# Low parts handed round between DMA, GpSimd and VectorE, and a first norm without GpSimd

## The chip, the cores and the metric

One core of a Trainium2 chip runs the whole program. The metric is device time in microseconds, the median of three runs. A core has five engines with a queue each: TensorE (PE, matrix products), VectorE (DVE), ScalarE (ACT), GpSimd (POOL) and SyncE (SP, which here only issues transfers); sixteen DMA engines carry the transfers.

## The reference

A trunk of two layers over 256 tokens of width 1024, in float32. Each layer does, with shift, scale and gate vectors from a conditioning vector c:

```
mod = silu(c) @ w_mod[l] + b_mod[l]                 # 6 vectors of 1024
h = rms_norm(x, norm1_g[l]) * (1.0 + sc1) + sh1
x = x + g1 * hybrid_mixer(h, ...)                   # attention, two convolutions, spatial gating; w_in, w_out
h = rms_norm(x, norm2_g[l]) * (1.0 + sc2) + sh2
x = x + g2 * peer_ffn(h, wq, keys, u, v)            # top 16 of 16384 experts per head, 8 heads
```

`peer_ffn` is computed densely: gelu(h @ u) for all 16384 experts, times gates that are zero for experts not picked, times v. Each layer reads 64 MB of u and 64 MB of v for it. A last rms_norm follows.

## The kernel before, in words

**Tiles and parts.** All weights come as a stream of 128x1024 tiles of 512 KB (20 of w_in, 8 of w_out, 16 of wq, 128 of u and 128 of v a layer). TensorE multiplies in a rounded float32 format, so each tile is split into a high part (its rounding) and a low part (the rest), and each product is made of three: high by high, high by low and low by high (`mm3`, lines 362 to 364). The activations are split in the same way. A tile of u, w_in or wq takes 8 chunks x 3 = 24 matmuls of 256 columns (`products`), a tile of v 12 of 512 columns (`down`, line 928).

**The stream** (`Stream`, lines 154 to 217). `load` issues the transfer of a tile from SP into one of four buffers `raw` (line 175). `split_halves` splits half a tile at a time, 128x512, into `hi` and `lo`, six buffers each. The low part is made in one of three ways. By VectorE or GpSimd: ScalarE writes the high part (line 200), and the engine subtracts it from raw (line 202). By DMA: ScalarE writes the negated high part into `lo` (line 196), GpSimd issues a transfer that adds the raw tile onto it (line 197), and ScalarE writes the high part (line 198). Which way a tile goes is set by `share`, a dictionary of fractions that are summed up tile by tile; what is left goes to VectorE. After the second half of tile n is split, `load(n + 4)` is called; that transfer waits until nothing reads the buffer of tile n any more. `ahead` keeps the splitting five halves ahead of the products.

**Shares.** The mixers and the query projection use `MIXSHARE` (DMA 0.4). `SHARE` has four entries for the expert stage: the first 64 tiles of u, the second 64, the first 64 tiles of v, the second 64 (`experts`, lines 954 to 969).

**Work beside the products.** `Background` holds generators, and after each tile `pump` takes slices from them as long as a plan of VectorE's load allows (2.6 us of plan for each tile, line 933 and others; a low half on VectorE is charged with 0.6, line 204). In the first half of "up" these are the top-k search of the experts (`topk`; line 799 adds two score lists, 792 is its last search step, 815 to 821 build one-hot tables), and in layer 0 then 16 modulation tiles. In the second half of "up" and in "down" the gates follow (`gates`, line 879), and in layer 0 during "down" 40 modulation tiles of layer 1. The framework's own scheduler orders each engine's instructions afterwards, so the order of issue is not that of the source.

**Modulation** (`mod_tiles`, lines 273 to 295). The vectors are sums along rows: a 128x1025 tile of w_mod is loaded by SP (line 280), and VectorE multiplies it by silu(c) and sums it (line 286). `n` buffers are used in turn; a slice of the generator is one sum.

**The start** (`start`, lines 1021 to 1084). The first norm needs the statistics of x (`rstd_d`) and 16 modulation tiles, taken one by one. GpSimd multiplies x by the reciprocal root (line 1060), ScalarE applies scale and shift twice, once rounded (1067) and once not (1069), and GpSimd subtracts (1073); the last chunk goes by VectorE. The first two weight tiles have their low parts made by DMA (`share = {"dma": 1.0}`, `split(1)`). In the later norms (`norm_mod`, lines 348 to 353) VectorE scales (350), ScalarE rounds (351) and VectorE makes the low part (352).

Of the kernel before, what the change touches and what calls it, by code (L numbers as in the profile page):

```python
# [10 lines left out]
F32 = mybir.dt.float32  # L11
# [3 lines left out]
AF = mybir.ActivationFunctionType  # L15
ALU = mybir.AluOpType
# [4 lines left out]
T = 256  # L21
L = 2
NC = D // P
# [14 lines left out]
MODCOST = 1.2  # L38
LOCOST = 0.6
HALF = D // 2  # L40
# [5 lines left out]
KTAKE = 3  # L46
CONVRANK = 2.5
PACE = (1.0, 2.6)
SHARE = ({"dma": 0.3, "pool": 0.7}, {"dma": 0.25}, {"dma": 0.2}, {"dma": 0.1})
NCOL = 94  # L50
NROW = 64 + 256 + 256 + 128
CH_SLICES = (4, 3, 0, 1, 7, 6, 5)
# [101 lines left out]
class Stream:  # L154
# [24 lines left out]
    def split_halves(self, upto):  # L179
        nc = self.nc  # L180
        while self.ns <= min(upto, 2 * len(self.aps) - 1):
            n, k = divmod(self.ns, 2)
            if k == 0:
                self.load(n)
                self.parts[n] = ([], [])
                self.by = "dve"
                for way in ("dma", "pool"):
                    self.acc[way] += self.share.get(way, 0.0)
                    if self.by == "dve" and self.acc[way] >= 1.0:
                        self.acc[way] -= 1.0  # L190
                        self.by = way
            raw = self.raw[n][:, HALF * k:HALF * k + HALF]
            hi = self.pool.tile([P, HALF], F32R, name="hi", tag="hi", bufs=6)
            lo = self.pool.tile([P, HALF], F32R, name="lo", tag="lo", bufs=6)
            if self.by == "dma":
                nc.scalar.activation(out=lo, in_=raw, func=AF.Copy, scale=-1.0)  # L196
                nc.gpsimd.dma_start(out=lo, in_=raw, accum_op=ALU.add)  # L197
                nc.scalar.activation(out=hi, in_=raw, func=AF.Copy)  # L198
            else:
                nc.scalar.activation(out=hi, in_=raw, func=AF.Copy)  # L200
                eng = nc.gpsimd if self.by == "pool" else nc.vector
                eng.tensor_tensor(out=lo, in0=raw, in1=hi.bitcast(F32), op=ALU.subtract)  # L202
                if self.by == "dve":
                    self.bg.charge(LOCOST)
            self.parts[n][0].append(hi)
            self.parts[n][1].append(lo)
            self.ns += 1
            if k:
                del self.raw[n]
                self.load(n + self.depth)  # L210
# [9 lines left out]
class Trunk:  # L220
# [52 lines left out]
    def mod_tiles(self, l, chunks, sc, bufs, tail=True, pace=0.0):  # L273

        nc = self.nc
        n = len(bufs)

        def load(i):
            if i < len(chunks):
                nc.sync.dma_start(out=bufs[i % n], in_=self.io["wmod"][l, chunks[i]])  # L280

        for i in range(n - 1):
            load(i)
        for i, j in enumerate(chunks):
            w = bufs[i % n]
            nc.vector.scalar_tensor_tensor(out=w, in0=w, scalar=1.0, in1=sc, op0=ALU.mult, op1=ALU.mult,  # L286
                                           accum_out=self.modT[:, l, j:j + 1])
            load(i + n - 1)
            yield MODCOST, pace
        for j0 in (8, 32):  # L290
            if tail and j0 in chunks:
                m = self.modT[:, l, j0:j0 + 8]
                g = self.col(l, 0 if j0 == 8 else 8, 8)
                nc.vector.scalar_tensor_tensor(out=m, in0=m, scalar=1.0, in1=g, op0=ALU.add, op1=ALU.mult)
                yield 0.2
# [64 lines left out]
    def mm3(self, out, whi, wlo, hhi, hlo, start, stop):  # L360
        mm = self.nc.tensor.matmul
        mm(out, whi, hhi, start=start, stop=False)  # L362
        mm(out, whi, hlo, start=False, stop=False)  # L363
        mm(out, wlo, hhi, start=False, stop=stop)  # L364
# [574 lines left out]
    def experts(self, l, area):  # L939
# [13 lines left out]
        acts = [self.big(32, T) for _ in range(2)]  # L953
        self.stream.share = SHARE[0]
        run = self.up(hb, acts)
        next(run)
        self.stream.share = SHARE[1]
        acts += [self.big(32, T) for _ in range(2)]
# [5 lines left out]
        for i in range(2):  # L964
            self.bg.add(self.gates(1, acts[2:4], i, kept))
        self.stream.share = SHARE[2]
        run = self.down(acts)
        next(run)
        self.stream.share = SHARE[3]
        self.m = Carve(self.big(), self.big())  # L970
# [50 lines left out]
    def start(self):  # L1021

        nc, io, one = self.nc, self.io, self.one
        self.cols = one.tile([P, L * NCOL + 8], F32, name="cols")
        self.ident = one.tile([P, P], F32, name="ident")
        self.xT = one.tile([P, NC, T], F32, name="xT")
        self.ones = one.tile([P, P], F32, name="ones")
        self.eps = one.tile([P, 1], F32, name="eps")
        self.iota = one.tile([P, P, 2], FP16, name="iota")
        self.modT = one.tile([P, L, 48], F32, name="modT")  # L1030
        self.idx = one.tile([P, 2, T], FP16, name="idx")
        self.gidx = one.tile([P, 2 * T], FP16, name="gidx")
        nc.vector.memset(self.ones, 1.0)
        nc.vector.memset(self.eps, EPS)
        self.neghalf = one.tile([P, 8], F32, name="neghalf")
        nc.vector.memset(self.neghalf, -0.5)
        self.m = m = Carve(self.big(), self.big())
        self.m2 = Carve(self.big())
        row = m.take(D)
        nc.sync.dma_start(out=row[0:1], in_=io["crow"])  # L1040
        nc.sync.dma_start(out=self.cols, in_=io["cols"])
        for i in range(2):
            nc.sync.dma_start(out=self.xT[:, 4 * i:4 * i + 4], in_=io["xT"][:, 4 * i:4 * i + 4])
        cr = self.m2.take(D + 1)
        for i in range(2):
            b = self.bank()
            nc.tensor.matmul(b, self.ones[0:1], row[0:1, 512 * i:512 * i + 512], start=True, stop=True)
            nc.scalar.activation(out=cr[:, 512 * i:512 * i + 512], in_=b, func=AF.Silu)
        nc.vector.memset(cr[:, D:D + 1], 1.0)
        bufs = [self.m2.take(D + 1) for _ in range(6)]  # L1050
        mods = self.mod_tiles(0, [j for c in range(NC) for j in (c, 8 + c)], cr, bufs, tail=False)
        next(mods)
        rs = self.rstd_d(m)
        self.stream.depth = 0
        self.stream.share = {"dma": 1.0}
        self.stream.split(1)
        r = self.bias_rows()
        xa, a = m.take(NC, T), m.take(2, T)
        for c in range(NC):
            nc.gpsimd.tensor_tensor(out=xa[:, c], in0=self.xT[:, c], in1=rs, op=ALU.mult)  # L1060
        hhi, hlo = hb = [self.mid(NC, T, dt=F32R) for _ in range(2)]
        for c in range(NC):
            for _ in range(2 if c else 1):
                next(mods)
            sh, sc = self.modT[:, 0, c:c + 1], self.modT[:, 0, 8 + c:9 + c]
            nc.vector.tensor_scalar(out=sc, in0=sc, scalar1=1.0, scalar2=self.col(0, c, 1), op0=ALU.add, op1=ALU.mult)
            nc.scalar.activation(out=hhi[:, c], in_=xa[:, c], func=AF.Identity, scale=sc, bias=sh)
            if c < NC - 1:
                nc.scalar.activation(out=a[:, c % 2], in_=xa[:, c], func=AF.Identity, scale=sc, bias=sh)
            else:  # L1070
                nc.vector.tensor_scalar(out=a[:, c % 2], in0=xa[:, c], scalar1=sc, scalar2=sh, op0=ALU.mult, op1=ALU.add)
            eng = nc.gpsimd if c < NC - 1 else nc.vector
            eng.tensor_tensor(out=hlo[:, c], in0=a[:, c % 2], in1=hhi[:, c].bitcast(F32), op=ALU.subtract)  # L1073
        for _ in mods:
            pass
        self.stream.load(3)
        self.stream.depth = self.stream.RAW
        nc.sync.dma_start(out=self.ident, in_=io["consts"][:, 0:P])
        m.reset()
        self.bias = m.take(4, 256)  # L1080
        self.table = self.bg.add(self.bias_table(r), rank=-1)
        self.bg.pump(0.1)
        self.mods = self.mod_tiles(0, list(range(16, 40)), cr, bufs[0:WBUFS])
        return hb
# [101 lines left out]
```

## Time and profile before

| | |
|---|---|
| median of 3 runs | 2087.24 us (2086.33 to 2091.59) |
| profiled execution | 2079.62 us, span 2077.8 us, mean granted clock 0.961 |
| busy share of the span | PE 92%, PE weight load 83%, DVE 69%, ACT 56%, POOL 26% |
| low parts | DMA 290 halves, GpSimd 178, VectorE 732 |
| DMA | 485.59 MB, 234 GB/s; q1 (plain loads) 56.9% and q0 (GpSimd's) 20.9% of 16 engines |

A busy share is a mean over stages with different limits; the stages are told apart by windows, given in us from the start of the span. In a wait, "A <- B" says that A was idle until B was done. "Up" is the product with u, "down" that with v.

### The profile page before, as it was taken

The page shows a single profiled execution, that of the slowest core. Times are in us where ns is not written, and L with a number is a line of the kernel's source. Part 1 is how long each engine was busy: PE and PEld are TensorE (multiplying, and loading weights), DVE is VectorE, ACT ScalarE, POOL GpSimd, SP SyncE. Part 2 cuts the span into 40 slices and gives each one's busy share as a digit, 9 for nine tenths or more (in the row PEclk, how much of TensorE's full clock was granted, in tenths as well). Part 3 has the DMA queues.
Part 4 walks back from the last instruction along what each step waited for, and adds up shares of the span by engine and source line. Part 5 has one row for each costly group of instructions (what it writes and reads, how often), then busy time and mean ns, then how long its engine had stood idle before and what let it go on. Part 6 is the DMA issues. An engine that isn't in the chain of part 4 may idle for free. (4 is left out here: it accounts for less than half of the span.)

```text
span 2077.8 us, 38198 instructions
## 1 busy us (share of the span) xinstructions
PE 1908.0 (92%) x13718; PEld 1720.2 (83%) x13718; DVE 1432.6 (69%) x3280; ACT 1155.0 (56%) x2329; POOL 537.2 (26%) x513
## 2 busy tenths in 40 slices
PE   4877987899999998889999989999999999999998
PEld 3777887889999886667787889999999988878886
DVE  6787799344666687666557877993477668855555
ACT  4565653465555554444557776666555555555554
POOL 4121265772111110000002223777411111110001
PEclk7988998899999999999999999999999999999999
DMA  8886877887888888898766767887888788877673
GB/s 289 256 254 204 223 198 223 260 229 218 249 244 255 255 256 287 279 295 284 225 211 168 206 167 204 238 219 219 234 262 243 245 255 271 261 207 220 210 212 113
DMA packets 164735, 485.59 MB, mean 234 GB/s; under 512 B 18588, under 2 KB 19905, under 8 KB 164290
## 3 DMA queue, kind: packets, MB, share of 16 engines
q1 hardware_dynamic: 122786, 407.13, 56.9%
q0 software_dynamic: 41760, 76.04, 20.9%
q8 instruction: 107, 1.75, 0.3%
q14 instruction: 82, 0.67, 0.1%
HBM read 388.72 MB, written 18.36 MB: 196 GB/s over the span
## 5 line engine op out<-in xcount | busy, mean ns | idle before, releaser
L364 PE MATMUL bank<-mid,lo 128*128 128x256 f32 x2432 | 702.3, 289 | 61.1 <-DMA lo<-raw 59.1
L200 ACT ACTIVATE hi<-raw 128x512 fp32r<-128x512 f32 x910 | 543.6, 624 | 323.4 <-PE bank L363 192.5
L362 PE MATMUL bank<-mid,hi 128*128 128x256 f32 x2432 | 704.5, 290 | 13.5 <-ACT hi L200 6.7
L363 PE MATMUL bank<-mid,hi 128*128 128x256 f32 x2432 | 695.5, 286 | 8.9 <-POOL mid L1073 8.9
L202 DVE TENSOR_TENSOR lo<-raw,hi 128x512 fp32r<-128x512 f32 x732 | 485.0, 688 | 204.5 <-ACT hi L200 200.1
L197 POOL DMA_DIRECT2D lo<-raw x290 | 253.2, 894 | 1390.6 <-PE acc L928 651.6
L928 PE MATMUL acc<-hi,mid 128*128 128x512 f32 x2048 | 570.0, 396 | 0.1
L364 PEld LDWEIGHTS bank<-mid,lo 128*128 128x128 f32 x2432 | 474.8, 195 | 72.0 <-DMA lo<-raw 69.2
L362 PEld LDWEIGHTS bank<-mid,hi 128*128 128x128 f32 x2432 | 475.1, 196 | 18.1 <-ACT hi L200 7.1
L363 PEld LDWEIGHTS bank<-mid,hi 128*128 128x128 f32 x2432 | 475.3, 196 | 9.5 <-POOL mid L1073 9.2
L928 PEld LDWEIGHTS acc<-hi,mid 128*128 128x128 f32 x2048 | 386.2, 191 | 78.4 <-ACT mid L913 0.4
L928 PE MATMUL acc<-lo,mid 128*128 128x512 f32 x1024 | 328.4, 398 | 31.5 <-DMA lo<-raw 31.2
L913 ACT ACTIVATE mid<-big 128x256 fp32r<-128x256 f32 x256 | 106.0, 415 | 307.8 <-PE acc L928 307.2
L928 PEld LDWEIGHTS acc<-lo,mid 128*128 128x128 f32 x1024 | 195.0, 190 | 84.5 <-DMA lo<-raw 44.2
L202 POOL TENSOR_TENSOR lo<-raw,hi 128x512 fp32r<-128x512 f32 x178 | 249.9, 1516 | 45.1 <-ACT hi L200 42.1
L198 ACT ACTIVATE hi<-raw 128x512 fp32r<-128x512 f32 x290 | 181.3, 625 | 134.7 <-PE bank L363 65.3
L914 DVE TENSOR_TENSOR mid<-big,mid 128x256 fp32r<-128x256 f32 x256 | 107.8, 423 | 199.0 <-PE acc L928 143.2
L196 ACT ACTIVATE lo<-raw 128x512 fp32r<-128x512 f32 x290 | 179.4, 621 | 57.8 <-PE acc L928 50.1
L286 DVE SCALAR_TENSOR_TENSOR big<-big 128x1025 f32<-128x1025 f32 x96 | 128.9, 1352 | 64.1 <-DMA big<-wmod 56.5
L874 DVE TENSOR_TENSOR og<-o,gidx 128x512 f16<-128x512 f16 x256 | 101.5, 436 | 0.2
L898 ACT ACTIVATE big<-bank 128x256 f32<-128x256 f32 x256 | 93.9, 367 | 0.0
L879 PEld LDWEIGHTS <-o 128*128 128x128 f16 x2048 | 67.4, 97 | 18.6 <-issue 12.3
(203 smaller groups left out, 1617.0 us busy)
## 6 DMA issues: line engine op xcount, KB each, us to landing
raw<-u SPq DMA_DIRECT2D x256, 512.0 KB, 4.6
raw<-v SPq DMA_DIRECT2D x256, 512.0 KB, 4.4
lo<-raw POOLq DMA_DIRECT2D x290, 256.0 KB, 5.0
big<-wmod SPq DMA_DIRECT2D x96, 512.5 KB, 6.5
raw<-win SPq DMA_DIRECT2D x40, 512.0 KB, 4.7
raw<-wq SPq DMA_DIRECT2D x32, 512.0 KB, 4.4
kept<-o SPq DMA_DIRECT2D x64, 256.0 KB, 5.2
o<-kept SPq DMA_DIRECT2D x64, 256.0 KB, 4.5
```

Source lines behind the costliest of these rows:

```text
L196: nc.scalar.activation(out=lo, in_=raw, func=AF.Copy, scale=-1.0)
L197: nc.gpsimd.dma_start(out=lo, in_=raw, accum_op=ALU.add)
L198: nc.scalar.activation(out=hi, in_=raw, func=AF.Copy)
L200: nc.scalar.activation(out=hi, in_=raw, func=AF.Copy)
L202: eng.tensor_tensor(out=lo, in0=raw, in1=hi.bitcast(F32), op=ALU.subtract)
L286: nc.vector.scalar_tensor_tensor(out=w, in0=w, scalar=1.0, in1=sc, op0=ALU.mult, op1=ALU.mult, accum_out=self.modT[:, l, j:j + 1])
L362: mm(out, whi, hhi, start=start, stop=False)
L363: mm(out, whi, hlo, start=False, stop=False)
L364: mm(out, wlo, hhi, start=False, stop=stop)
L913: nc.scalar.activation(out=a[:, 0], in_=src, func=AF.Copy)
L914: nc.vector.tensor_tensor(out=a[:, 1], in0=src, in1=a[:, 0].bitcast(F32), op=ALU.subtract)
L928: nc.tensor.matmul(self.acc[2 * tt + d], a[:, s, P * tt:P * tt + P], w[:, 512 * d:512 * d + 512], start=i == 0 and s == 0 and w is whi, st ...
```

## The change

Four edits. The shares of the expert stage change. A low part made by DMA adds the tile as it lies in HBM (`self.aps[n]`), not the raw buffer. In `mod_tiles` the load of a later tile is issued after the `yield`, so with the next slice. And the first norm is written like the later ones, VectorE scaling and making the low part, ScalarE rounding, with the shift added on the way; the first two weight tiles are loaded ahead and split inside its loop over the eight chunks, after chunks 2 and 4, with no share, so by VectorE.

```diff
-SHARE = ({"dma": 0.3, "pool": 0.7}, {"dma": 0.25}, {"dma": 0.2}, {"dma": 0.1})
+SHARE = ({"pool": 0.6}, {"dma": 0.25}, {"dma": 0.15}, {})
...
                 nc.scalar.activation(out=lo, in_=raw, func=AF.Copy, scale=-1.0)
-                nc.gpsimd.dma_start(out=lo, in_=raw, accum_op=ALU.add)
+                nc.gpsimd.dma_start(out=lo, in_=self.aps[n][:, HALF * k:HALF * k + HALF], accum_op=ALU.add)
                 nc.scalar.activation(out=hi, in_=raw, func=AF.Copy)
...
                                            accum_out=self.modT[:, l, j:j + 1])
+            yield MODCOST, pace
             load(i + n - 1)
-            yield MODCOST, pace
...
-        self.stream.share = {"dma": 1.0}
-        self.stream.split(1)
+        self.stream.share = {}
+        self.stream.load(1)
         r = self.bias_rows()
-        xa, a = m.take(NC, T), m.take(2, T)
-        for c in range(NC):
-            nc.gpsimd.tensor_tensor(out=xa[:, c], in0=self.xT[:, c], in1=rs, op=ALU.mult)
+        a = m.take(2, T)
...
-            nc.scalar.activation(out=hhi[:, c], in_=xa[:, c], func=AF.Identity, scale=sc, bias=sh)
-            if c < NC - 1:
-                nc.scalar.activation(out=a[:, c % 2], in_=xa[:, c], func=AF.Identity, scale=sc, bias=sh)
-            else:
-                nc.vector.tensor_scalar(out=a[:, c % 2], in0=xa[:, c], scalar1=sc, scalar2=sh, op0=ALU.mult, op1=ALU.add)
-            eng = nc.gpsimd if c < NC - 1 else nc.vector
-            eng.tensor_tensor(out=hlo[:, c], in0=a[:, c % 2], in1=hhi[:, c].bitcast(F32), op=ALU.subtract)
+            t = a[:, c % 2]
+            nc.vector.scalar_tensor_tensor(out=t, in0=self.xT[:, c], scalar=sc, in1=rs, op0=ALU.mult, op1=ALU.mult)
+            nc.scalar.activation(out=hhi[:, c], in_=t, func=AF.Identity, bias=sh)
+            if c in (2, 4):
+                self.stream.split(c // 2 - 1)
+            nc.vector.scalar_tensor_tensor(out=hlo[:, c], in0=t, scalar=sh, in1=hhi[:, c].bitcast(F32), op0=ALU.add,
+                                           op1=ALU.subtract)
```

## Rows read from the trace of the kernel before

**Rows 1.** Windows by stage: us, busy us (instructions) by engine, clock, DMA share, GB/s

```profile
254.00:371.00 117.00, 98.28 (x737) 95.72 (x736) 111.12 (x318) 55.42 (x112) 70.16 (x59) 0.91 0.74 217
371.00:483.00 112.00, 97.22 (x759) 95.80 (x758) 39.30 (x44) 60.32 (x117) 79.55 (x67) 0.94 0.82 233
784.00:985.00 201.00, 174.41 (x819) 137.41 (x818) 139.34 (x277) 93.89 (x188) 15.52 (x18) 0.93 0.88 289
1281.00:1378.00 97.00, 94.62 (x783) 93.77 (x782) 93.70 (x320) 60.08 (x116) 71.80 (x63) 1.00 0.82 226
1378.00:1477.00 99.00, 93.49 (x758) 92.37 (x757) 51.06 (x53) 60.72 (x117) 77.09 (x63) 0.98 0.82 226
1477.00:1690.00 213.00, 211.51 (x2126) 209.44 (x2125) 136.34 (x286) 119.48 (x237) 34.93 (x39) 1.00 0.81 248
1783.00:1941.00 158.00, 156.34 (x805) 126.70 (x804) 95.36 (x186) 89.45 (x183) 15.70 (x18) 1.00 0.76 224
```

**Rows 2.** Windows, two stretches in which TensorE has no gap

```profile
1425.00:1445.00 20.00, 19.96 (x165) 19.65 (x165) 4.05 (x5) 13.67 (x29) 16.06 (x14) 1.00 0.81 220
1950.00:2000.00 50.00, 50.00 (x219) 40.79 (x219) 29.40 (x53) 28.64 (x59) 3.08 (x4) 1.00 0.72 212
```

**Rows 3.** TensorE's waits, layer 0, first half of "up": total us, times, longest

```profile
PE bank L364 <- DMA lo<-raw: 25.4, 13, 5.8
PE bank L362 <- ACT hi L200: 6.7, 2, 5.1
```

**Rows 4.** TensorE's waits, layer 1, first half of "up"

```profile
PE bank L364 <- DMA lo<-raw: 7.7, 7, 2.0
```

**Rows 5.** Waits of all engines in the stretch of layer 0's "down"

```profile
PE acc L928 <- DMA lo<-raw: 26.6, 17, 3.6
DVE big L286 <- DMA big<-wmod: 26.6, 18, 4.1
```

**Rows 6.** Line 197 in that stretch: its issues, and its transfers

```profile
L197 POOL DMA_DIRECT2D lo<-raw x18: 859/862/877, 792.8 to 961.0; - x18
...
DMA to landing us min/median/max: 5.0/8.0/9.4
```

**Rows 7.** SP's waits, whole span

```profile
SPq L175 <- DMA lo<-raw: 693.4, 132, 13.4
```

**Rows 8.** SP's waits, first 32 tiles of layer 0's "up"

```profile
SPq L280 <- DVE big L792: 31.1, 3, 17.2
```

**Rows 9.** Line 286 (modulation sums), layer 0's "down": ns min/median/max, first and last start

```profile
L286 DVE SCALAR_TENSOR_TENSOR big<-big x40: 1217/1222/1229, 792.3 to 985.5; 128x1025 f32<-128x1025 f32 x40
```

**Rows 10.** Line 350 (scaled norm, 128x256), both layers

```profile
L350 DVE SCALAR_TENSOR_TENSOR big<-xT,modT,big x24: 475/479/484, 198.9 to 1247.5; 128x256 f32<-128x256 f32 x24
```

**Rows 11.** Page, part 5: low halves on VectorE: busy us, mean ns, idle before

```profile
L202 DVE TENSOR_TENSOR lo<-raw,hi 128x512 fp32r<-128x512 f32 x732 | 485.0, 688 | 204.5 <-ACT hi L200 200.1
```

**Rows 12.** TensorE's timeline at the start: start us, us, [idle before <-releaser]

```profile
31.89 0.58 PE L363 MATMUL bank<-mid,hi 128*128 128x256 f32 x1 [8.94 <-POOL mid L1073]
38.19 0.58 PE L364 MATMUL bank<-mid,lo 128*128 128x256 f32 x1 [5.71 <-DMA lo<-raw]
```

**Rows 13.** ScalarE's timeline: first activation of the first product

```profile
48.72 0.38 ACT L627 ACTIVATE big<-bank 128x256 f32<-128x256 f32 x1 [4.81 <-PE bank L364]
```

**Rows 14.** GpSimd's timeline: four low halves, layer 1

```profile
1294.79 5.35 POOL L202 TENSOR_TENSOR lo<-raw,hi 128x512 fp32r<-128x512 f32 x4
```

**Rows 15.** VectorE's timeline: the top-k addition alone and beside them

```profile
1292.16 0.41 DVE L799 TENSOR_TENSOR big<-big 128x256 f32<-128x256 f32 x1
...
1295.76 4.67 DVE L799 TENSOR_TENSOR big<-big 128x256 f32<-128x256 f32 x1
```

**Rows 16.** Groups of VectorE, layer 1, first half of "up"

```profile
L799 DVE TENSOR_TENSOR big<-big 128x256 f32<-128x256 f32 x16 | 34.2, 2139 | 0.0
```

**Rows 17.** Line 197, layer 1, second half of "up": who waited, and landing

```profile
  PE bank L364: 1.4, 3
...
DMA to landing us min/median/max: 3.3/5.3/6.9
```

## The prediction

> **What bounds the kernel now.** I first read the window table by stage: TensorE's busy time, the granted clock and the DMA share of each stretch, one layer beside the other, since both do the same products. [rows 1] holds the stretches that differ. The first half of the expert up-projection (64 tiles, cut here at the 32nd tile's activation) takes 117 + 112 = 229 us in layer 0 and 97 + 99 = 196 us in layer 1. A stretch of some 56 tiles of the down-projection (819 and 805 matmuls) takes 201 us in layer 0 and 158 us in layer 1. The second half of the up-projection has TensorE busy in 211.5 of 213 us. What is the least? Where TensorE runs without a gap, 165 products of 256 columns take 20 us and 219 of 512 columns take 50 us [rows 2]: 0.121 us and 0.228 us each, so an up tile (24 products) takes 2.91 us, a down tile (12) 2.74 us, and 64 up tiles 186 us. So layer 1 is bound by TensorE almost everywhere (196 against 186), and layer 0 loses 43 us in the first half of "up" and 43 us in the down stretch. That is what a change can win.
>
> Next the table of waits, by window, says what TensorE waited for there: in layer 0's half "up" 25.4 us for low parts that a DMA makes and 6.7 us for high parts [rows 3], in layer 1 7.7 us [rows 4]; in the down stretch 26.6 us for low parts by DMA, 17 times [rows 5], which is nearly each of the 18 halves made so there; they landed after 8.0 us in the median [rows 6]. The granted clock of 0.93 [rows 1] means 14% of 201 us at the lower of its two levels (1.2 of 2.4 GHz), half of which, 14 us, is lost: 26.6 + 14 explains the 43. Last come the waits of SP, whose queue issues all plain loads in order: 693.4 us in 132 waits for a raw tile that a low-part DMA still reads [rows 7], and, in layer 0's half "up", 31.1 us in three waits of a modulation load for a top-k step on VectorE (L792), all tile loads being queued behind it [rows 8].
>
> **The change, part by part.** The sum is made against the profiled execution, 2079.62 us, which lies 7.6 us under the median of 2087.24; I add these 7.6 at the end.
>
> *Start.* VectorE takes over all of the norm. Its work from 8.70 us on: 16 sums over modulation tiles at 1.22 [rows 9] and 0.08, 16 operations on 128x256 at 0.48 [rows 10] (eight scaled, eight low parts), 4 low halves at 0.69 [rows 11], and 4 us of reciprocal, copy and scales: 20.8 + 7.7 + 2.8 + 4 = 35.3, and about 2.7 of waiting for the statistics, less some 3 of overlap between neighbours. The last low part is out near 43.7 us, six products and the activation follow, near 45.5. Today the first product waits 8.94 us for GpSimd's low part and 5.71 us for the DMA's [rows 12], and its activation starts at 48.72 [rows 13]. I take -3 (between -6 and +2, since VectorE becomes the only bound).
>
> *First half of "up", low parts from DMA 0.3 / GpSimd 0.7 to GpSimd 0.6 / VectorE 0.4.* The waits for DMA go: 25.4 and 7.7. What is late next? GpSimd does four halves in 5.35 us [rows 14], so 1.34 each: its load falls from 0.7 x 2 x 1.34 + 0.3 x 2 x 0.86 (issue, [rows 6]) = 2.4 us to 1.6 us a tile of 2.91, and no longer bounds. VectorE gets 51 halves a layer. In the first 32 tiles it is already busy 93.7 of 97 us [rows 1] with top-k, and its queue is in order: a low half stands behind the top-k steps issued before it, and TensorE waits for it once the lead of five halves (5 x 1.45 = 7 us) is used up. The 26 halves there cost 26 x 0.69 = 18 us [rows 11], and each may wait for the port: a 128x256 addition of 0.41 us took 4.67 us [rows 15] while GpSimd ran its four halves, and 2.14 us in the mean of 16 [rows 16], 1.73 above 0.41. So the wait w per half lies between 0 and 1.7; I take 0.5, nearer to 0, since GpSimd has pauses at 1.6 of 2.91 us where today it runs in chains. The 16 additions then get 16 x 1.2 = 20 us back. VectorE needs 93.7 + 18 + 13 - 20 = 105 us, against 32 x 2.91 = 93 and 7 of lead: 5 us late. In the second 32 tiles VectorE is busy 51 of 99 us, so the halves fit, but they stand behind one-hot steps of 2 to 3 us in a row; I add one lead, 7. Drag: 12 us a layer. Its ends: 0 (w = 0), and 57 + 7 = 64 (w = 1.7).
> The Trainium skill (SBUF — State Buffer, section Who interferes with whom) says that a VectorE instruction with two SBUF inputs and a GpSimd instruction that reads SBUF take a port by turns, the later one blocking for the length of the other. By that, w would stay under one GpSimd half and average about 0.4, the drag would be 7, and the sum 10 us lower. The trace shows a wait through a chain of four, longer than the rule, so I keep the row.
> Layer 0: 186 + 6.7 + 4 (half clock around these waits) + 12 = 209, so -20. The SP stall stays in it (no load of the first three moves), but with VectorE and TensorE tied together it should not grow. Layer 1: 186 + 2 + 12 = 200, so +4.
>
> *Down, DMA 0.2 / 0.1 to 0.15 / 0.* In the stretch of rows 5 the first 32 tiles keep 4.8 DMA tiles, the other 24 have none: 10 halves of 18. Waits 26.6 x 10/18 = 15, clock 14 x 10/18 = 8: 18 us gained. The DMA engines (0.88 busy, [rows 1]) lose 8 slow halves of work and raw tiles come free earlier: 6 more. -24, between -8 (the 40 modulation loads in this stretch only fill the room) and -43 (all of layer 1's speed). VectorE takes these halves at 0.69 us; it is busy 139 of 201 us, which hides it. The rest of both down stages: -2.
>
> *The DMA reads the tile from HBM, not from the raw buffer.* 172 of 290 halves stay with DMA (0.4 x 44, 0.25 x 64 and 0.15 x 64 tiles a layer). A raw buffer is free once ScalarE has copied it, so SP's 693 us shrink; TensorE sees little of that, since it waits 1.4 us in all of layer 1's second "up" half [rows 17]. But the load that was held back until the low part had landed now runs beside it. Best, the waits of these stages that are left, some -30; worst, every later half of 81 tiles waits as in rows 5, 1.5 us: +121. The row nearest is that of the same stage: landing up to 6.9 us with 1.4 us of waits [rows 17]; a little later does little. I take +5.
>
> *Modulation loads issued after the yield.* One slice later in SP's order, ahead of the next sum. Queued behind a load that waits are the tile loads; behind a sum that waits, VectorE's low parts. Sums waited 26.6 us for loads in the down stretch [rows 5], with VectorE idle 62 us there: 0, between -10 (less blocking of SP) and +27 (the waits double and reach TensorE).
>
> Sum: -3 - 20 + 4 - 24 - 2 + 5 = -40. 2079.6 - 40 + 7.6 = 2047 us.
>
> **The rivals.**
> *All covers hold.* No drag, no collision, and the down stretch becomes like layer 1's: -5 at the start, 229 + 196 - 2 x 188 = -49, -43, and -6 elsewhere: -103, 1984 us. For it: GpSimd's relief; against: VectorE full for 97 us.
> *The port makes it slower.* VectorE's halves wait as the additions do today. Each 0.1 us of w costs (26 + 16) x 0.1 = 4.2 us a layer, 8.4 in both, so from w = 1.0 on the gain is gone. At 1.25, half way to the row's end, +63: 2110 us; at 1.7, 2150. For it: [rows 15, 16]; against: GpSimd's load falls by a third.
> *Low parts by DMA land later* because raw loads run beside them and the second read is a read of HBM under 250 GB/s. If a third of the 162 halves outside the down stretch waits 1.5 us: +80, 2127 us. For it: 8.0 us of landing where traffic is dense [rows 6]; against: 5.3 us in "up" [rows 17]. The Trainium skill (HBM Reference, section Latency) puts an access at 0.2 us on average and at 2 us under high load; by its upper figure such a half would land at 7.3 us and most would be late by little. No run here shows it.
> *Nothing moves.* The order in which instructions are issued is not that of the source (the 40 modulation sums that the code adds after tile 64 of "down" begin at 792 us, [rows 9], some 30 tiles earlier), so the redistribution may only trade DMA waits for VectorE waits: w = 1.0, 2089 us.
>
> **How the numbers follow.** Forecast 0.55 (2047, its own range 2015 to 2072), all covers 0.13, nothing moves 0.13, the port 0.11, DMA later 0.08. The bound between a change and none is 0.3%, 6 us: 2081 to 2093.5. Of "nothing moves" 0.09 lies inside and 0.02 on either side. Faster 0.55 + 0.13 + 0.02 = 0.70, same 0.09, slower 0.19 + 0.02 = 0.21. The range 2000 to 2105 leaves out about 0.09 below and 0.11 above.
>
> **What would show it.** Right: the first activation of the first layer near 45.5 us; no wait for DMA low parts in the first half of "up", layer 0's half near 209 us and layer 1's near 200; the down stretch near 177 us with its clock above 0.96; SP's waits for low parts by DMA under a third. Wrong: TensorE waiting for VectorE's low parts by more than 30 us a layer, the 128x256 additions still at 2 us, low parts by DMA landing at 7 us or more in the second half of "up", or the down stretch still near 200 us.

## The result, and the profile after

The kernel became slower: 2113.79 us (median of 4 runs, 2103.76 to 2122.67) against 2087.14 us, a ratio of 1.012 with a 95% interval of 1.007 to 1.017. The forecast was 2047 us, in a range of 2000 to 2105: wrong in sign, and outside its range. The profiled execution of after is its slowest one, 2122.67 us with a span of 2120.9, which is 43.1 us over the span before; the medians differ by 26.7.

First the same stages as in [rows 1], after. The columns are start and end, length, TensorE's busy time, weight loads, VectorE, ScalarE, GpSimd, the granted clock, the DMA share and GB/s.

```profile
240.00:448.00 208.00, 191.83 (x1533) 188.49 (x1532) 184.63 (x413) 100.66 (x197) 125.80 (x76) 0.98 0.60 204
768.00:955.00 187.00, 166.66 (x795) 133.42 (x795) 141.11 (x272) 88.38 (x178) 8.86 (x11) 0.95 0.87 295
1278.00:1480.00 202.00, 188.30 (x1531) 185.53 (x1529) 152.13 (x380) 101.32 (x197) 115.61 (x77) 0.99 0.51 169
1480.00:1701.00 221.00, 205.68 (x2032) 201.34 (x2031) 136.62 (x285) 112.33 (x220) 25.90 (x30) 0.98 0.78 227
1701.00:1920.00 219.00, 199.62 (x1250) 159.14 (x1247) 143.22 (x320) 101.52 (x208) 16.56 (x20) 0.95 0.68 204
```

The first three are the stages that the change was aimed at. Layer 0's first half of "up" takes 208 us (forecast 209), layer 1's takes 202 (forecast 200): so far the forecast holds. The down stretch takes 187 (forecast 177, before 201), some half of the gain that was forecast. The last two rows are stages in which I had expected next to nothing. Layer 1's second half of "up" took some 201 us before between the same two activations, bound by TensorE ([rows 1] has a longer cut of it, 213 us); it now takes 221. The first half of its "down" took 187 and now takes 219, with the clock down from 1.00 to 0.95. These two alone lose 52 us. The first half of layer 1's "down" in the kernel before:

```profile
1690.00:1877.00 187.00, 185.54 (x1236) 150.21 (x1236) 138.83 (x314) 102.71 (x212) 21.99 (x26) 1.00 0.82 246
```

TensorE's longest waits, whole span (total us, times, longest):

```profile
PE acc L928 <- DMA lo<-v: 41.9, 23, 3.7
PE bank L364 <- DVE lo L202: 30.4, 28, 3.5
PE bank L364 <- DMA lo<-u: 22.5, 20, 3.0
PE bank L364 <- DMA lo<-win: 13.1, 7, 5.7
PE bank L364 <- DMA lo<-wq: 10.2, 6, 4.9
```

Four of the five rows are low parts made by DMA, 87.7 us in 56 waits (smaller rows bring it to 93.3 us in 60). They bear the names of the weights (u, v, win, wq), since the transfer now reads those in HBM. What does the transfer itself look like? Line 197 in the last two stages above, first "up", then "down": who waited for it, and the time from issue to landing, as in [rows 17].

```profile
L197 POOL DMA_DIRECT2D lo<-u x30: 862/862/865, 1490.6 to 1689.6; - x30
...
  PE bank L364: 14.2, 11
...
DMA to landing us min/median/max: 3.8/6.3/9.3
```

```profile
L197 POOL DMA_DIRECT2D lo<-v x20: 862/865/1219, 1704.6 to 1919.9; - x20
...
  PE acc L928: 15.8, 10
...
DMA to landing us min/median/max: 3.5/7.0/8.6
```

In "up" the median landing rose from 5.3 to 6.3 us and the longest from 6.9 to 9.3, and TensorE's waits rose from 1.4 us in 3 to 14.2 in 11. (These two rows follow the transfers that were issued in the window; counted by the time of the wait, as in the table of stages below, it is 15.1 in "up" and 13.5 in "down".) One microsecond was the whole slack.

Last, the wait that the new source was to take away, in SP's queue [rows 7]:

```profile
SPq L175 <- DVE lo L202: 987.9, 361, 12.8
SPq L175 <- POOL lo L202: 95.3, 44, 5.0
SPq L175 <- ACT lo L196: 81.8, 41, 3.7
```

It is gone: no row names a DMA's low part. SP now waits until VectorE has read the raw tile, and no longer until the DMA has. And the second read of 172 halves (172 x 262,144 bytes = 45.1 MB) shows in the page, first before, then after:

```profile
HBM read 388.72 MB, written 18.36 MB: 196 GB/s over the span
```

```profile
HBM read 433.81 MB, written 18.36 MB: 213 GB/s over the span
```

### The profile page after: what moved, and what is told of

Read it like the earlier page. It is cut to its first block, busy times and chain, and to the rows that moved or that the text cites. A ratio compares the mean times of both kernels' runs of the same rounds, so it can differ in the third digit from the quotient of the medians.

```text
span 2120.9 us, 37761 instructions
## 1 busy us (share of the span) xinstructions
PE 1930.9 (91%) x13718; PEld 1736.4 (82%) x13718; DVE 1509.3 (71%) x3438; ACT 1101.6 (52%) x2208; POOL 417.5 (20%) x354
## 4 chain that ended last, share of the span: by engine, by line
PE 40%; issue 23%; DMA 13%; DVE 12%; POOL 1%; ACT 1%; POOLq 0%; DVEq 0%; SPq 0%; ACTq 0%
PE acc L928 17%; PE bank L364 7%; DMA lo<-u 7%; PE bank L362 7%; PE bank L363 7%; DMA lo<-v 3%; DVE lo L202 2%; DMA lo<-wq 1%; DMA lo<-win 1%; POOL lo L197 1%; DVE big L789 1%; PE acc L879 1%; DVE big L818 1%; DVE big L790 1%; DVE big L792 1%
## 5 line engine op out<-in xcount | busy, mean ns | idle before, releaser
L202 DVE TENSOR_TENSOR lo<-raw,hi 128x512 fp32r<-128x512 f32 x876 | 610.7, 721 | 287.4 <-ACT hi L200 282.7
L928 PE MATMUL acc<-hi,mid 128*128 128x512 f32 x2048 | 577.2, 400 | 0.1
L928 PEld LDWEIGHTS acc<-hi,mid 128*128 128x128 f32 x2048 | 391.1, 193 | 80.6 <-ACT mid L913 0.4
L202 POOL TENSOR_TENSOR lo<-raw,hi 128x512 fp32r<-128x512 f32 x152 | 244.1, 1618 | 177.1 <-ACT hi L200 157.0
L286 DVE SCALAR_TENSOR_TENSOR big<-big 128x1025 f32<-128x1025 f32 x96 | 123.6, 1293 | 38.8 <-DMA big<-wmod 38.6
L197 POOL DMA_DIRECT2D lo<-u x66 | 57.1, 865 | 381.5 <-ACT lo L196 193.1
L196 ACT ACTIVATE lo<-raw 128x512 fp32r<-128x512 f32 x172 | 105.8, 621 | 28.3 <-PE acc L928 25.0
L197 POOL DMA_DIRECT2D lo<-v x40 | 34.6, 872 | 431.9 <-PE acc L928 331.9
L874 DVE TENSOR_TENSOR og<-o,gidx 128x512 f16<-128x512 f16 x256 | 96.4, 417 | 0.2
```

The lines of the kernel that those rows point to most:

```text
L197: nc.gpsimd.dma_start(out=lo, in_=self.aps[n][:, HALF * k:HALF * k + HALF], accum_op=ALU.add)
L928: nc.tensor.matmul(self.acc[2 * tt + d], a[:, s, P * tt:P * tt + P], w[:, 512 * d:512 * d + 512], start=i == 0 and s == 0 and w is whi, st ...
```

## The experiments

My theory after the result: the place from which the low-part DMA reads costs some 70 us, and the rest of the change gains about what was forecast. The rivals were that VectorE and GpSimd hold each other up (theory 2 in the expectations), or that the new start or the moved modulation loads cost something (theory 3 is the loads). All ratios are against the kernel before, run on the same chip in turn (its medians: 2089.65, 2086.4 and 2089.39 in the three groups).

### One part alone, and the change without it

**The source alone** (`src_alone`): the kernel before, with only line 197 changed, so that all its 290 halves by DMA read HBM.

```
-                nc.gpsimd.dma_start(out=lo, in_=raw, accum_op=ALU.add)
+                nc.gpsimd.dma_start(out=lo, in_=self.aps[n][:, HALF * k:HALF * k + HALF], accum_op=ALU.add)
```

> Only the source of the adding transfers is changed (HBM instead of the raw buffer), all 290 halves. Theory 1 (the second read from HBM makes these halves land later and TensorE waits for them): landing in the second half of up from 5.3 to 6.4 us or more, TensorE's waits for low parts by DMA from 97 us to 150 or more, time 2110 to 2160. Theory 2 (the redistribution pushes low parts and gates back on VectorE, the source costs nothing): 2075 to 2095, waits as before. Theory 3 (the modulation loads): 2087.

**The change without it** (`undo_src`): the same line, the other way round, in the kernel after.

> The changed kernel with the source put back to the raw buffer, the other three edits kept. Theory 1: the loss of the second half of up (+20 in layer 1) and of the first half of down (+32 in layer 1) goes, 2035 to 2065, about what was forecast without a cost of the source. Theory 2: it stays, 2100 to 2115. Theory 3: it stays too.

**The redistribution alone** (`share_alone`), and **the first norm alone** (`start_alone`, the start block of the diff), each in the kernel before:

```
-SHARE = ({"dma": 0.3, "pool": 0.7}, {"dma": 0.25}, {"dma": 0.2}, {"dma": 0.1})
+SHARE = ({"pool": 0.6}, {"dma": 0.25}, {"dma": 0.15}, {})
```

> Only the four shares are changed, source still the raw buffer. Theory 1: first half of up in layer 0 from 229 to about 208 us, in layer 1 about +5, down in layer 0 shorter by 15 to 25: 2045 to 2075. Theory 2: 2100 to 2120, with waits of TensorE for VectorE's low parts above 30 us and a slower second half of up. Theory 3: 2045 to 2087.

> Only the first norm is changed. All theories: first product's activation 3 to 5 us earlier, 2078 to 2086; if the gain of the first mixer (18 us by its last matmul in the changed kernel) is due to the start, 2065 to 2075.

Measured (us):

| kernel | median | range | ratio (95%) |
|---|---|---|---|
| src_alone | 2226.66 | 2214.77–2232.87 | 1.065 (1.060–1.069) |
| undo_src | 2044.62 | 2039.97–2049.75 | 0.977 (0.973–0.982) |
| share_alone | 2062.32 | 2055.20–2071.09 | 0.986 (0.982–0.990) |
| start_alone | 2078.07 | 2067.89–2087.03 | 0.994 (0.991–0.997) |

The source costs 2226.66 - 2089.65 = 137 us with 290 halves, well above the 2110 to 2160 us that were expected, and 2113.79 - 2044.62 = 69 us with 172 (about 73 by the two ratios to the kernel before). The two other parts gain 27.3 and 11.6 us alone, and 45.0 together: within their intervals they add up. Without the source the change is a gain of 2.3%.

What TensorE sees of the source, in `src_alone`, to be held against the waits of after:

```profile
PE acc L928 <- DMA lo<-v: 84.5, 62, 3.8
PE bank L364 <- DMA lo<-u: 66.1, 54, 6.0
PE bank L364 <- DMA lo<-win: 22.6, 5, 8.4
PE bank L364 <- DMA lo<-wq: 13.3, 6, 5.1
```

That is 186.5 us; before, the same table has these two rows, 90.3 us:

```profile
PE bank L364 <- DMA lo<-raw: 59.1, 36, 5.9
PE acc L928 <- DMA lo<-raw: 31.2, 23, 3.6
```

So 96 us more of waiting. The span is 135.2 us longer (2213.0 against 2077.8). The rest is the clock: the mean granted clock is 0.946 against 0.961, and (1 - clock) x span, the work that TensorE did not get, is 119.5 us against 81.0, 38.5 more. 96 + 38.5 = 134.7. The two terms overlap (time that TensorE waits at the lower clock is in both), so the agreement is better than the reckoning; read directly, TensorE was busy 45.2 us longer with the same 13718 instructions (1953.1 against 1908.0). From `undo_src` to after the same sum is 46.4 us of waits (87.7 against 41.3) and 95.4 - 65.2 = 30.2 us of clock (0.955 against 0.968), 76.6 of the 82.7 us between the spans.

### Is it the read of HBM, or the loads that it sets free?

Two things change with the source. The second read comes from HBM; and a raw buffer is free sooner, so that the next raw load leaves while the low part is still in flight. Three experiments try to part them.

**Holding the loads by a small transfer** (`src_hold`): `src_alone`, and before a raw buffer is given up, four bytes go from the low part into it on SP's queue, so that the next load comes after the landing.

```
+                if self.by == "dma":
+                    nc.sync.dma_start(out=self.raw[n][0:1, 0:1], in_=self.parts[n][1][1][0:1, 0:1].bitcast(F32))
```

> Source in HBM as in the run with the source alone, but the raw buffer of such a tile is held until its low part has landed, as it is when the transfer reads the buffer: a 4-byte transfer in SP's queue from the low part into the raw tile stands ahead of the next load (it adds some 2 us to that load's wait). Theory 1a (a read from HBM takes longer to land than one from the buffer): no better than with the source alone, 2200 to 2250, median landing in the second half of up 6.3 us or more. Theory 1b (the raw loads that are no longer held back run beside the low parts and delay them): back near the kernel before or a little above for the 4-byte transfers, 2090 to 2140, landing 5.0 to 5.6 us.

Measured: 2192.11 us, ratio 1.049 (1.047–1.052), within neither of the two ranges that were expected. As built it tells little. The small transfer takes time of its own in SP's queue, 0.59 us to issue each of the 145 and 75.4 us of waiting for them, which lengthens the way round the raw buffers: layer 1's second half of "up" took 218.9 us, longer than in `src_alone` (210.9), while the two halves of its "down" came down from 217.6 and 205.3 to 193.0 and 189.4.

**Holding them without it** (`src_held`): `src_alone`, and each raw load waits for the low parts of its buffer's last tile by an added dependency. SP's order and what it waits for are then those of before, and only the place that the DMA reads is another.

```
-            self.nc.sync.dma_start(out=t, in_=self.aps[self.nd])
+            ins = self.nc.sync.dma_start(out=t, in_=self.aps[self.nd])
+            for low in self.lows.pop(self.nd - self.RAW, ()):
+                self.tc.add_manual_dep(ins.ins, low.ins.name, mybir.DependencyInfo(mybir.DependencyClass.Sync, mybir.DependencyReason.DATA), reason="hold")
...
```

> Source in HBM for all 290 halves, and each raw load waits for the low parts of the tile whose buffer it takes, by an added dependency and nothing else: SP's order and its waits are those of the kernel before, only the place that the transfer reads differs. Theory 1a (the read from HBM itself): near the run with the source alone, 2190 to 2230, the lowest landing 0.7 us above the kernel before and the medians in layer 1's down 6.5 us or more. Theory 1b (the raw loads set free collide with the low parts): 2085 to 2110, medians in layer 1's down 4.9 to 5.5 us. Both by halves: 2130 to 2170, medians between.

Measured: 2129.66 us (2121.37–2136.52), ratio 1.019 (1.016–1.023). With the wait back, 97 of the 137 us are gone. The other 40 us stay with the read of HBM. SP's waits show that the loads are held again:

```profile
SPq L175 <- DMA lo<-u: 517.7, 69, 9.9
SPq L175 <- DVE lo L204: 337.6, 176, 7.9
SPq L175 <- DMA lo<-v: 254.0, 38, 10.0
SPq L175 <- DMA lo<-win: 106.9, 17, 10.1
SPq L175 <- DMA lo<-wq: 85.7, 12, 15.5
```

They are held longer than before: with 44.2 us in 6 waits for w_out, 1008.5 us in 142 waits against 693.4 in 132 [rows 7], and the low parts land later: the median over the whole kernel is 5.0 us before, 5.9 in `src_held` and 6.6 in `src_alone`. Whatever the longer hold costs is in the 40 us; TensorE's waits for anything but low parts did not grow (57.4 us, before 61.4). The split also goes by this order, first the read of HBM and then the loads. Loads set free beside a read of the raw buffer were not tried, and in the stage below the first 1.2 us of later landing cost 3.4 us of waits, the next 1.4 us 16.0.

One stage shows both parts side by side, the first half of layer 1's "down", 26 halves by DMA in each of the three kernels. The transfers of `before`, `src_alone` and `src_held` (the line is L199 there):

```profile
L197 POOL DMA_DIRECT2D lo<-raw x26: 869/872/1220, 1689.3 to 1875.5; - x26
...
  PE acc L928: 0.7, 2
...
DMA to landing us min/median/max: 3.3/4.2/5.2
```

```profile
L197 POOL DMA_DIRECT2D lo<-v x26: 872/872/1227, 1772.3 to 1988.9; - x26
...
  PE acc L928: 20.1, 18
...
DMA to landing us min/median/max: 4.0/6.8/8.7
```

```profile
L199 POOL DMA_DIRECT2D lo<-v x26: 872/872/1227, 1722.6 to 1912.2; - x26
...
  PE acc L931: 4.1, 6
...
DMA to landing us min/median/max: 3.5/5.4/6.5
```

The HBM read adds 1.2 us to the median landing, the loads beside it another 1.4. TensorE, which has some slack, feels the second part far more: 0.7, then 4.1, then 20.1 us of waits, for stages of 187, 191 and 218 us. Not every stage is like this one. In the first half of layer 1's "up" TensorE waits 7.7 us for low parts by DMA before, 18.8 in `src_held` and 20.7 in `src_alone`: there holding the loads gave next to nothing back.

How many loads fly beside a low part? I counted in the traces, for each low part by DMA, the 512 KB loads that SP issued between 1.5 us before its issue and 1.5 us before its landing. The mean is 0.56 before, 0.60 in `src_held`, 1.96 in `src_alone`, 2.01 after and 0.50 in `undo_src`. The median landing in us by that number, with the count of low parts:

| loads beside | before | src_held | src_alone | after |
|---|---|---|---|---|
| 0 | 4.7 (170) | 5.6 (182) | 4.8 (12) | 3.9 (2) |
| 1 | 5.4 (83) | 5.9 (62) | 5.1 (63) | 5.1 (39) |
| 2 | 7.0 (32) | 6.9 (25) | 6.6 (146) | 6.6 (90) |
| 3 | 8.3 (5) | 7.5 (21) | 7.5 (63) | 7.7 (37) |
| 4 | | | 8.2 (6) | 8.5 (4) |

At an equal number of loads the four kernels lie within about a microsecond of each other (but for a group of two low parts); the number of loads is what moved. (A transfer that takes longer also has more time to meet loads, so the table shows that they go together; that the loads are a cause is shown by `src_held`.)

**The transfer by itself** (`probe_landing`): the kernel before, with 32 low parts by DMA added after the last norm, one at a time, eight of each kind: source in the raw buffer or in HBM, alone or beside two raw loads. It adds work, so its total says nothing.

> The kernel before with 32 adding transfers of one half tile after the last norm, one after another: 8 from the raw buffer and 8 from HBM with nothing beside them, then 8 and 8 with two raw loads issued beside each. Time some 150 to 250 us above the kernel before. Theory 1a: the HBM ones land at least 0.4 us later than the others, alone and beside loads. Theory 1b: equal within 0.2 us when alone, both 1 to 2.5 us later beside loads.

One execution, 2258.82 us. Landings in order: from HBM beside loads, from the raw buffer beside loads, from the raw buffer alone, from HBM alone (L1101 is the transfer). The scheduler issued the loads earlier than the source has them, so that of the sixteen from the raw buffer the last three ran alone, and the five ahead of these beside loads in a steady rhythm; the first eight were irregular (3.3 to 7.4 us) and are not used. "Beside loads" is one or two: behind each low part SP issued one load after some 0.25 us, and behind six of the eight from HBM and two of the five from the raw buffer a second one.

```profile
L1101 POOL DMA_DIRECT2D lo<-wout x8: 863/872/884, 2113.6 to 2159.4; - x8
...
DMA to landing us min/median/max: 5.5/5.6/5.7
```

```profile
L1101 POOL DMA_DIRECT2D lo<-raw x5: 869/869/877, 2165.9 to 2193.5; - x5
...
DMA to landing us min/median/max: 5.8/5.9/6.2
```

```profile
L1101 POOL DMA_DIRECT2D lo<-raw x3: 869/869/869, 2200.4 to 2208.8; - x3
...
DMA to landing us min/median/max: 3.3/3.3/3.3
```

```profile
L1101 POOL DMA_DIRECT2D lo<-wout x8: 872/872/877, 2213.1 to 2247.8; - x8
...
DMA to landing us min/median/max: 3.9/4.0/4.1
```

Alone, the read of HBM lands 0.7 us later. Beside loads there is no such difference (5.6 against 5.9): from HBM it is 1.6 us later than alone, from the raw buffer 2.6. The company costs more than the source. Neither of the two expectations came: HBM was later alone, but not beside loads.

The Trainium skill (HBM Reference, section Latency) gives an access 0.2 us on average and 2 us under high load. Of its upper figure these rows show nothing: the extra was 0.7 us alone and none beside one or two loads.

### The other parts, and a better version

**The place of the modulation loads** (`undo_src_yield`): `undo_src` with the load ahead of the yield again.

```
+            load(i + n - 1)
             yield MODCOST, pace
-            load(i + n - 1)
```

> The changed kernel with the source back in the raw buffer and the modulation loads issued before the yield again. If the place of these loads costs nothing, as forecast: the time of the run with the source undone, 2037 to 2052. Theory 3 (they matter): more than 10 us away from it, with VectorE's waits for modulation tiles and SP's for VectorE's sums changed by as much.

Measured: 2040.57 us (2033.78–2049.71), ratio 0.979 (0.976–0.982), against 0.977 (0.973–0.982) without this edit. No difference that can be told.

**No DMA low parts in "down" at all** (`undo_src_down0`):

```
-SHARE = ({"pool": 0.6}, {"dma": 0.25}, {"dma": 0.15}, {})
+SHARE = ({"pool": 0.6}, {"dma": 0.25}, {}, {})
```

> The changed kernel with the source back in the raw buffer and no low parts by DMA in all of down (0 instead of 0.15 in its first half). TensorE's waits for them in down, 21.5 us with the source undone, go; VectorE takes 38 more halves of 0.69 us beside the gates. If these waits are the price: 2020 to 2040. If VectorE's queue is then late: 2045 to 2060, with waits for its low parts in the first half of down.

Measured: 1999.58 us (1995.11–2008.02), ratio 0.960 (0.957–0.962): 45 us below `undo_src`, below both kernels of the case, and below both ranges that were expected. The stretch of [rows 1, 5] now runs with hardly a gap and at the full clock, in 166 us, with the DMA engines busier than ever:

```profile
738.00:904.00 166.00, 164.90 (x869) 134.04 (x868) 149.54 (x299) 86.50 (x175) 0.00 (x0) 1.00 0.90 318
```

In `undo_src` the same stretch still takes 191 us at a clock of 0.94:

```profile
745.00:936.00 191.00, 169.76 (x804) 135.62 (x803) 141.26 (x274) 90.31 (x182) 9.46 (x11) 0.94 0.87 289
```

Eleven halves by DMA were left there. The two windows are not cut at quite the same product. Over the same 56 tiles, from the first product of the 30th tile to that of the 86th, it is 200.8 us before, 190.6 in `undo_src` and 161.5 here; layer 1 took 161.1 for them before (the 158 in [rows 1] holds 14 products fewer). The eleven halves and the lower clock that went with their waits cost 29 us; VectorE, busy 150 of 166 us now, makes them beside its other work.

From here two further steps on the same path: a smaller DMA part in the mixer (`down0_mix02`, MIXSHARE 0.4 to 0.2), and more of the first half of "up" on GpSimd (`down0_pool7`, 0.6 to 0.7), each in `undo_src_down0`:

```
-MIXSHARE = {"dma": 0.4}
+MIXSHARE = {"dma": 0.2}
```

```
-SHARE = ({"pool": 0.6}, {"dma": 0.25}, {}, {})
+SHARE = ({"pool": 0.7}, {"dma": 0.25}, {}, {})
```

> The best version so far (source in the raw buffer, no low parts by DMA in down) with the mixers' and queries' share by DMA cut from 0.4 to 0.2. If a low part by DMA costs more than one on VectorE there too: the 19 us of waits for DMA low parts in the mixers and queries go, 1980 to 1995. If VectorE's other work in the mixers hides nothing more: 1998 to 2015.

> The best version so far with the first half of up at GpSimd 0.7 and VectorE 0.3 instead of 0.6 and 0.4. If VectorE's lateness there (28 us of TensorE waits for its low parts) comes from the number of halves: waits down by a quarter or more, 1985 to 1997. If it comes from GpSimd holding VectorE up, more halves on GpSimd make it worse: 2000 to 2015.

Measured: 2008.11 us, ratio 0.960 (0.957–0.963), and 2001.09 us, ratio 0.958 (0.955–0.961). Neither gains. With 0.7 on GpSimd TensorE's waits for VectorE's low parts in the first half of "up" did not fall: one execution of each has 15.6 and then 19.8 us in layer 0, 12.7 and then 15.4 in layer 1, so that what delays VectorE's halves there is not their number alone.

## Why the prediction was wrong, step by step

All stages in one table (us; the stages are cut at the same activations, or nearly the same products, in each kernel, and the numbers in brackets are TensorE's waits for low parts by DMA). Each column is one execution, with spans of 2077.8, 2120.9, 2038.2 and 1993.0 us. Small differences say little: the stages of `probe_landing`, which up to its last norm is the kernel before, differ from the first column by up to 6 us, and the border between the halves of "down" lies within 18 products of the same place, which moves up to 7 us from one half to the other.

| stage | before | after | undo_src | undo_src_down0 |
|---|---|---|---|---|
| mixer and queries, layer 0, from 18 us on | 236.9 (22.4) | 222.5 (13.8) | 221.7 (10.6) | 221.3 (12.4) |
| up, 1st half, layer 0 | 233.6 (25.4) | 207.9 (0) | 207.9 (0) | 207.4 (0) |
| up, 2nd half, layer 0 | 202.8 (2.0) | 211.4 (7.4) | 203.7 (2.6) | 200.1 (0) |
| down, 1st half, layer 0 | 218.3 (17.5) | 223.2 (22.1) | 212.7 (17.8) | 188.6 (0) |
| down, 2nd half, layer 0 | 196.0 (12.2) | 187.3 (4.0) | 186.1 (3.4) | 180.7 (0) |
| mixer and queries, layer 1 | 187.3 (6.8) | 207.7 (15.0) | 196.5 (8.6) | 192.3 (6.8) |
| up, 1st half, layer 1 | 195.4 (7.7) | 202.3 (0) | 202.7 (0) | 202.0 (0) |
| up, 2nd half, layer 1 | 201.4 (1.4) | 221.0 (15.1) | 202.6 (2.1) | 200.3 (0.8) |
| down, 1st half, layer 1 | 187.2 (0.7) | 219.2 (13.5) | 189.8 (0) | 184.6 (0) |
| down, 2nd half, layer 1 | 183.3 (0.8) | 183.2 (2.4) | 179.2 (0.3) | 180.4 (0) |

**The failed step is "The DMA reads the tile from HBM": +5 forecast, +69 measured.** The text had the mechanism in view ("the load that was held back until the low part had landed now runs beside it") and then priced it by one row: landing up to 6.9 us with 1.4 us of waits, hence "a little later does little". That row shows the edge of the slack, not slack. Three waits of some 30 halves mean that the slowest tenth was already late; shift all by a microsecond, and eleven of thirty are late. A price should have come from the row next to it: 8.0 us of landing with a wait on 17 of 18 halves [rows 5, 6], one microsecond and a half per wait. It stood in the text as the worst case (+121). And the best case, "a raw buffer is free sooner", had no gain to give: SP's 693 us were no loss of TensorE's, but what kept loads and low parts apart (with the wait back, `src_held` is 97 us below `src_alone`).

The rival **"Low parts by DMA land later"** (2127 us, 0.08) was the right one, in mechanism and nearly in size: it put a third of 162 halves at 1.5 us, 80 us in all. After, TensorE waited 87.7 us in 56 waits, 1.6 us each, where `undo_src` has 41.3; the granted clock added 30 us. So the 80 us were 46 of waits and 30 of clock, which the rival had left out: that its size came near is partly luck. That both of its causes act is shown by `src_held`: some 30% is the read of HBM, 70% the loads beside it, of the 137 us with 290 halves, in the order tried. How the 69 us with 172 halves split was not tried.

**The sum of the rest held by luck, through errors that cancel.** Without the +5 the forecast is 2042 us; `undo_src` measured 2044.6. Its terms:

*Start, -3; alone it measured -11.6.* The first activation is close to the forecast of 45.5: 44.35 us with this part alone, 43.00 after, against 48.72 in [rows 13].

```profile
43.00 0.38 ACT L627 ACTIVATE big<-bank 128x256 f32<-128x256 f32 x1 [0.56 <-PE bank L364]
```

I stopped there. With this part alone, TensorE's waits for low parts by DMA in layer 0's mixer, the first product taken in, fell from 20.0 to 8.9 us; the 5.71 us at the first product is only half of that. What took the other waits away was not separated.

*First half of "up", -20 and +4; measured -25.7 and +6.9.* Right in both signs and near in size. (The 229 and 196 us before [rows 1] are not cut at the same products; from the first activation to the 65th it was 233.6 and 195.4.) The drag of 12 us a layer shows as TensorE's waits for VectorE's low parts, 16.2 and 13.7 us. The wait w for the port came out lower than the 0.5 us that I took. The groups of VectorE, layer 0 and then layer 1 (count, busy us, mean ns):

```profile
L202 DVE TENSOR_TENSOR lo<-raw,hi 128x512 fp32r<-128x512 f32 x52 | 52.8, 1032 | 15.9 <-ACT hi L200 15.9
...
L799 DVE TENSOR_TENSOR big<-big 128x256 f32<-128x256 f32 x16 | 11.3, 704 | 0.0
```

```profile
L202 DVE TENSOR_TENSOR lo<-raw,hi 128x512 fp32r<-128x512 f32 x51 | 45.4, 896 | 47.7 <-ACT hi L200 47.6
...
L799 DVE TENSOR_TENSOR big<-big 128x256 f32<-128x256 f32 x16 | 11.2, 700 | 0.0
```

Against the 688 ns of [rows 11] that is w = 0.34 and 0.21 us, and the additions fell from 2139 ns [rows 16] to 700. The Trainium skill (SBUF — State Buffer, section Who interferes with whom), by whose rule w was put at 0.4 and the drag at 7, is nearer than my 0.5 on w, but the drag was larger, not smaller. The place of the halves in VectorE's queue, which the text also had, is in it: each of the 27 halves that TensorE waited for started without a gap behind another VectorE instruction (top-k and one-hot steps, and in layer 0 modulation sums), and their own length above 688 ns makes up 8.4 of the 29.9 us. How much the port lengthened the instructions ahead of them was not separated.

*The down stretch, -24; measured about -10.* Without the new source the same 56 tiles take 190.6 us against 200.8, not 177. I had scaled waits and clock by the number of halves, 10 of 18. Eleven remained, and landed no sooner (8.8 us in the median of the stretch, before 8.0 [rows 6]); TensorE waited for each of them, 20.4 us in 11 waits where I had put 15. Fewer halves did not make the rest faster. The modulation loads beside them stayed, which may be why: in layer 1, with the same share and no such loads, low parts landed after 4.4 us and TensorE waited 0.3 us. No run took these loads away. `undo_src_down0` shows what was there to win, 39 us, by leaving no half to DMA.

*Layer 1's mixer and queries, not in the sum: +9.* Their shares did not change, yet `undo_src` takes 196.5 us there against 187.3. The waits for low parts by DMA grew by only 1.8 us of it, and the granted clock is 0.94 against 0.96. Why is open.

*Modulation loads after the yield, 0:* measured 0, within the interval.

Of the signs that I named for right, three came: the activation, the first half of "up", and SP's waits for low parts by DMA, which are gone; the down stretch stopped half way. Of the four named for wrong none came in full. The one that bore on the true cause, "low parts by DMA landing at 7 us or more in the second half of 'up'", was set too high: 6.3 us was enough. And none was named for layer 1's "down", where the most was lost.

## What to carry to other kernels

Price a wait that is taken away by what will then run beside the work that it held apart, above all in a queue that issues transfers in order; here 693 us of waiting in SP's queue protected the low parts. A transfer with few short waits has no slack left: read the whole distribution of landings against the lead, not the total of the waits. And where a few slow transfers hold a stage, taking all of them to an engine with room can be worth much more than taking half (here 39 us against 10).

## What the runs showed of the hardware that was not expected

- An adding transfer of 256 KB from the raw buffer landed after 3.3 us alone and 5.9 beside one or two loads of 512 KB; from HBM after 4.0 and 5.6. So the source showed only while the transfer was alone. In the kernel with the loads held, the read of HBM still cost 40 us, and in the first half of layer 1's "up" the median landing rose there from 4.9 to 6.5 us, more than 0.7; why is open.
- Short waits came with a lower clock: 96 us more of waits in `src_alone` came with 38.5 us more of work lost at the lower of the two levels (1.2 of 2.4 GHz). In layer 1's first half of "down" the granted clock was 1.00 before and 0.95 after, where TensorE waited 13.5 us in 8 waits for low parts and 5.8 us in 2 for a gate's transfer (o<-kept).
